# A hybrid attention encoder block on one core: the third block of projection weights is read into the room of the distance table, right behind the fourth tile of tokens

## The chip, the core and the metric

The program runs on one core of one Trainium2 chip, in one launch. Its engines each work through a queue of their own: PE (matrix products; PEld loads the stationary operand), DVE (VectorE), ACT (ScalarE), POOL (GpSimd) and SP (SyncE, which computes nothing here and issues all transfers between memory and on-chip buffers). They meet through semaphores. The metric is the device time of one execution in microseconds (us); lower is better.

## What is computed

One layer of an encoder over 1024 tokens of width 1024 with 16 meta tokens put in front. The part that matters here is the first stage: every token is normalised, and the result is multiplied by pieces of one large weight matrix.

```python
h = jnp.concatenate([meta, x], axis=1)
n = rms_norm(h, norm_mix[layer])
proj = n @ w_in[layer]
qb = proj[..., o:o + QB_W]; o += QB_W
kb = proj[..., o:o + KB_W]; o += KB_W
vb = proj[..., o:o + VB_W]; o += VB_W
y_a = differential_attention(qa, ka, va, ...)
y_b = windowed_gqa(qb, kb, vb, sink)
merged = sigmoid(ga) * (y_a @ w_ba) + sigmoid(gb) * (y_b @ w_bb)
h = h + merged @ w_o
h = h + swiglu(rms_norm(h, norm_ffn), w_gate, w_up, w_down)
```

## The kernel before

**Splitting.** Each float32 operand is split into a high part and a low part (`split`, L116: ACT copies the high part, L117; DVE or POOL subtracts it to get the low part, L118). A product is three passes of PE: high by high, low by high, high by low. The high and the low part of the normalised and transposed tokens stay on chip as `hT_hi` and `hT_lo`.

**The first stage.** There are eight tiles of 128 tokens, called tile 0 to tile 7 here after the buffers `x_0` to `x_7`, and a ninth with the 16 meta tokens. For each tile: `load_x` (L383) has SP issue a read of 512 KB; `norm_x` squares and sums the tile on ACT (L134), takes the root on POOL (L122, L123) and scales on DVE (L140); `turn_x` transposes on PE (L148, eight transposes in two banks) and splits on ACT (L150) and DVE (L151). The "fourth tile" of the title is `x_3`.

**The first three weight blocks.** A block is 128 columns of `w_in`, 512 KB: `kb` (read by `ensure` as `w_c2048`), the first half of `qb` (`w_c1536`), and the second half of `qb`, prepared at L434 under the name `qbx` into a tile of its own, `wb_qbx`, with its low part made on DVE. `project_steps` (L207) multiplies them by the tokens in four chunks of 256 tokens; a chunk needs two tiles. For each chunk PE makes 24 products for `kb` (`pp_kb`), 24 for the first half of `qb` (`pp_qb0`) and 24 for the second (`pp_qb1`), and the calls of `advance` mix these with the transposes of the later tiles. Every finished chunk is split (L232 to L236) and moved by SP to where the attention wants it: eight small transfers for `kb` (L282, sixteen for the last chunk), four for each half of `qb` (L305).

**Buffers.** `prep` (L174) reads a block into a tile of the pool `wpool`, tag `w`, which has two buffers. So the read of `qbx` takes the buffer of `w_c2048` when that has been split, the next block, `w_c2176` (for `vb`), the buffer of `w_c1536`, and the one after, `w_c0` (for the first `qa`), that of `qbx`. The table of distances `dist` (128 x 1920) is allocated and filled at L464 to L473, after all calls of `advance` in the text; DVE and POOL fill it while the projections run.

**After the stage** come the products for `vb` (`pp_vb`), the scores of the windowed attention (`attend_b`; products `bps` at L331, two banks of results, which DVE empties at L333), and the products for `qa` (`pp_qa`), mixed by the planner; then the differential attention, the gates, the output projection and the feed-forward part, which the change does not touch.

**What sets the order.** The instructions of this first part are not executed in the order of the text: a planner with a cost model of its own orders each engine's queue when the program is built. A change in the text can so move instructions it does not name. SP's transfers take eight semaphores in turn: a transfer is issued only after the one eight places ahead of it in the queue has landed. That can be seen where the order lists what an instruction waits for.

Of the kernel before, what the change touches and what calls it, by code (L numbers as in the profile page):

```python
# [9 lines left out]
F32 = mybir.dt.float32  # L10
# [9 lines left out]
P = 128  # L20
S = 1024
D = 1024
NM = 16
L = S + NM
DC = D // P
# [44 lines left out]
C_QA, C_KA, C_VA, C_QB, C_KB, C_VB, C_GA, C_GB = 0, 512, 1024, 1536, 2048, 2176, 2304, 3328  # L70
# [3 lines left out]
def encoder_block(ctx: ExitStack, tc: tile.TileContext, x, meta, norm_mix, w_in, lq1, lk1, lq2, lk2,  # L74
                  subln, sink, w_ba, w_bb, w_o, norm_ffn, w_g, w_u, w_d, norm_final, out, dbg=None):
    nc = tc.nc
    x = x[0]
    out = out[0]
    w_in, w_ba, w_bb, w_o = w_in[0], w_ba[0], w_bb[0], w_o[0]
# [5 lines left out]
    def pool(name, side="left", space=None, bufs=1):  # L85
        kw = {} if space is None else {"space": space}
        if space is not DRAM:
            kw["reuse_waits"] = "tile"
        cm = tc.tile_pool(name=name, bufs=bufs, side=side, **kw)
        p = cm.__enter__()  # L90
        return p, lambda: cm.__exit__(None, None, None)
# [24 lines left out]
    def split(hi, lo, src, lo_eng):  # L116
        nc.scalar.activation(hi, src, AF.Copy)  # L117
        lo_eng.tensor_tensor(lo, src, f32(hi), ALU.subtract)  # L118
# [12 lines left out]
    def normed(p, src, parts, gain, name, tag="xn", bufs=2, on_pool=False):  # L131
        xn = p.tile([P, D], F32, tag=tag, name=f"xn_{name}", bufs=bufs)
        ss = small.tile([P, 1], F32, tag="ss", name=f"ss_{name}")
        nc.scalar.activation(xn[:parts], src, AF.Square, accum_out=ss[:parts])  # L134
        r = rstd_of(ss[:parts], D, parts, f"rstd_{name}")
        if on_pool:
            nc.gpsimd.tensor_scalar(xn[:parts], src, r[:parts], 1.0, ALU.mult, ALU.mult)
            nc.gpsimd.tensor_tensor(xn[:parts], xn[:parts], gain[:parts], ALU.mult)
        else:
            nc.vector.scalar_tensor_tensor(xn[:parts], src, r[:parts], gain[:parts], ALU.mult, ALU.mult)  # L140
        return xn
# [11 lines left out]
    acon, close_acon = pool("acon", "right")  # L153
    hpool, close_hpool = pool("hpool", "right")
    wpool, close_wpool = pool("wpool", "right")
# [15 lines left out]

    queue = []

    def prep(col, name, p=None, lo_eng=None):  # L174
        w = wpool.tile([P, DC, P], F32, tag="w", name=f"w_{name}", bufs=2)
        if isinstance(col, tuple):
            for i, k in enumerate(col):
                nc.sync.dma_start(w[:, 4 * i:4 * i + 4], g_weights(k, 1, 0, P))
        else:
            nc.sync.dma_start(w, w_in[:, col:col + P].rearrange("(c p) n -> p c n", p=P))  # L180
        if p:
            both = p.tile([P, 2, DC, P], F32R, tag="k0", name=f"wb_{name}", bufs=1)
            wh, wl = both[:, 0], both[:, 1]
        else:
            wh = wpool.tile([P, DC, P], F32R, tag="wh", name=f"wh_{name}", bufs=W_BUFS)
            wl = wpool.tile([P, DC, P], F32R, tag="wl", name=f"wl_{name}", bufs=W_BUFS)
        split(wh, wl, w, lo_eng or nc.gpsimd)
        return wh, wl
# [9 lines left out]
    prepped = {}  # L198

    def ensure(n):  # L200
        while order and len(prepped) < n:
            col = order.pop(0)
            prepped[col] = prep(col, f"c{col[0] if isinstance(col, tuple) else col}", lo_eng=nc.vector if col in on_vector else None)
# [60 lines left out]
    lowpool, close_low = pool("lowpool")  # L264
# [115 lines left out]
    def load_x(t):  # L380
        xts[t] = bpool.tile([P, D], F32, tag="btr", name=f"x_{t}", bufs=4)
        if t < NT:
            nc.sync.dma_start(xts[t], x[t * P:(t + 1) * P, :])  # L383
        else:
            nc.sync.dma_start(xts[t][:NM], meta)

    def norm_x(t):
        parts = P if t < NT else NM
        i = len(done)
        done.append(t)  # L390
        p, tag, bufs = (vtpool, "vt", 1) if i % 3 == 2 else (bpool, "bs", 2)
        xns[t] = normed(p, xts.pop(t)[:parts], parts, gmix, f"a{t}", tag=tag, bufs=bufs)

    def turn_x(t):
        parts = P if t < NT else NM
        transposed(lambda name: bank(psum1, ("bt", "bs")[t % 2], name, 2), xns.pop(t), parts, hT_hi, hT_lo, t * P, f"a{t}")
# [29 lines left out]
        nc.tensor.matmul(idle, zeros[:, 0:P], zeros, start=True, stop=True)  # L426
    ensure(2)
    load_x(3)
    norm_x(2)
    turn_x(1)  # L430
    p_kb = project_steps(C_KB, KB_CHUNKS, "kb", evac_split(None, kb_consume))
    p_q0 = qb_steps(0, qb, 0)
    p_q1 = qb_steps(0, qb, 1)
    prepped[C_QB + P] = prep(C_QB + P, "qbx", lowpool, nc.vector)  # L434
    early += [(p_kb, DC), (p_q0, DC), (p_q1, DC)]
    advance(E_STEPS)
    norm_x(3)
# [23 lines left out]
    turn_x(NT)  # L461
    early += [(p_kb, DC), (p_q0, DC), (p_q1, DC)]
    advance(100)
    dist = acon.tile([P, 1920], F32, name="dist")  # L464
    tbx = acon.tile([P, 3, 144], F32, name="tbx")
    for i in range(2):
        cols = slice(960 * i, 960 * i + 960)
# [122 lines left out]
    def g_weights(k, kh, c0, cn):  # L590
        at = (C_GB, C_GA)[k // 4] + k % 4 * 256 + c0
        return w_in[kh * 512:kh * 512 + 512, at:at + cn].rearrange("(c p) n -> p c n", p=P)
# [430 lines left out]
    for o in range(DC):  # L1023
        w = first_w[o] if o < 2 else branch_w(ypool, o, w_bb, "b")
# [424 lines left out]
    for n in range(nf, len(steps)):  # L1449
        p, j = steps[n][1]  # L1450
# [3 lines left out]
        if p in LOADS:  # L1454
            at, half, col = LOADS[p]
# [62 lines left out]
```

## Time and profile before

| what | us |
|---|---|
| time, median of three runs | 1447.92 (1447.72 to 1450.47) |
| time of the profiled execution | 1446.43 |
| its span, first to last instruction | 1444.6 |
| PE busy | 1423.5 (99%) |
| DVE busy | 901.6 (62%) |
| ACT busy | 679.5 (47%) |
| POOL busy | 642.6 (44%) |
| mean granted clock of PE | 0.997 of full speed |

How to read it: the profiled execution is one execution, 1.5 us quicker than the median of the runs beside it, and 1.8 us longer than its own span. PE is busy nearly all the time, so what matters is where PE stands still and for whom. A row of the timeline has the start, the time taken, the engine, the line, the operation and its tiles (written <- read); in brackets the engine's idle time before it and what ended that. Products on PE overlap: the next one starts before the end that is shown for the last.

### The profile page before, as it was taken

To read this page: it belongs to the slowest core of one execution; us is meant where nothing else is said; L and a number is where in the kernel's file an instruction comes from. 1 tells how busy PE (TensorE), PEld (TensorE's weight loads), DVE (VectorE), ACT (ScalarE), POOL (GpSimd) and SP (SyncE) were. 2 spreads that over 40 slices of the span, in tenths; PEclk is the share of its full clock that TensorE was granted. 3 is DMA by queue.
4 is the path that set the end of the run, shared out by engine and by line. 5 is a ranking of instruction groups with operands and counts; after the bars stand their busy time and mean duration, and the time that the engine had idled before them with its cause. 6 is when DMAs were issued, how large, how long until landed. Compare 5 with 4: busy or idle time off the path is not lost.

```text
span 1444.6 us, 21159 instructions
## 1 busy us (share of the span) xinstructions
PE 1423.5 (99%) x7279; PEld 1221.1 (85%) x7279; DVE 901.6 (62%) x1624; ACT 679.5 (47%) x1290; POOL 642.6 (44%) x605
## 2 busy tenths in 40 slices
PE   8999999999999999999999999999999999999997
PEld 6988989988898989888888878888888888888886
DVE  7478536637697989624614966554555553787567
ACT  6356535545665656545413643333333333444454
POOL 5589227743333333334522665544544552000444
PEclk9999999999999999999999999999999999999999
DMA  8367668995558473586602534333332333964343
GB/s 245 87 211 231 195 160 271 283 289 208 189 168 258 147 226 126 190 255 204 224 32 88 152 103 162 110 102 110 101 103 96 110 102 102 334 205 140 124 130 139
DMA packets 188891, 242.41 MB, mean 168 GB/s; under 512 B 18208, under 2 KB 115936, under 8 KB 188784
## 3 DMA queue, kind: packets, MB, share of 16 engines
q1 hardware_dynamic: 188784, 241.07, 52.5%
q8 instruction: 57, 0.93, 0.3%
q14 instruction: 50, 0.41, 0.1%
HBM read 157.45 MB, written 77.00 MB: 162 GB/s over the span
## 4 chain that ended last, share of the span: by engine, by line
PE 80%; POOL 6%; DVE 5%; issue 4%; DMA 3%; ACT 2%; SPq 0%; POOLq 0%; DVEq 0%; ACTq 0%
PE pg L1299 27%; PE pd L1393 9%; PE pg L742 7%; PE ppa L786 6%; PE po L1076 6%; PE aps L802 3%; PE pp_qb L214 3%; PE apy L841 3%; POOL oa L118 3%; PE pp_ka L214 2%; PE pp_va L214 2%; PE apt L828 2%; PE pp_qa L214 2%; PE bpt L356 1%; PE bpy L362 1%
## 5 line engine op out<-in xcount | busy, mean ns | idle before, releaser
L118 POOL TENSOR_TENSOR wop<-wf,wop 128x512 fp32r<-128x512 f32 x128 | 173.5, 1360 | 164.7 <-ACT wop L117 150.3
L1299 PE MATMUL pg<-t,wop 128*128 128x512 f32 x1056 | 242.6, 389 | 0.0
L1299 PEld LDWEIGHTS pg<-t,wop 128*128 128x128 f32 x1056 | 198.2, 188 | 41.2
L1393 PE MATMUL pd<-ob,oa 128*128 128x512 f32 x924 | 209.9, 389 | 0.4 <-POOL oa L118 0.4
L1393 PEld LDWEIGHTS pd<-ob,oa 128*128 128x128 f32 x924 | 173.3, 188 | 36.8 <-POOL oa L118 0.9
L1299 PE MATMUL pg<-b,wop 128*128 128x512 f32 x792 | 185.6, 392 | 2.3 <-DVE c L1308 2.3
L1299 PEld LDWEIGHTS pg<-b,wop 128*128 128x128 f32 x792 | 149.4, 189 | 34.2 <-issue 2.4
L742 PE MATMUL pg<-hT_hi,gop 128*128 128x512 f32 x384 | 142.9, 397 | 0.0
L118 POOL TENSOR_TENSOR oa<-ra,oa 128x512 fp32r<-128x512 f32 x33 | 44.1, 1337 | 170.0 <-ACT oa L117 168.6
L117 ACT ACTIVATE wop<-wf 128x512 fp32r<-128x512 f32 x128 | 80.2, 631 | 83.3 <-PE pg L1299 47.8
L118 POOL TENSOR_TENSOR gop<-gr,gop 128x512 fp32r<-128x512 f32 x47 | 62.0, 1321 | 105.9 <-ACT gop L117 105.9
L117 ACT ACTIVATE oa<-ra 128x512 fp32r<-128x512 f32 x77 | 48.7, 632 | 106.1 <-PE pd L1393 46.0
L810 ACT ACTIVATE as<-as,amn 128x1040 f32<-128x1040 f32 x64 | 74.5, 1165 | 47.3 <-DVE amn L805 43.2
L1134 DVE TENSOR_TENSOR s<-wf,wf 128x512 f32<-128x512 f32 x22 | 23.7, 1077 | 107.6 <-DMA wf<-in_w_ff_gate_dram 57.4
L802 PE MATMUL aps<-ak,aq 128*128 128x392 f32 (+1 forms) x384 | 90.1, 330 | 0.7 <-DVE amn L805 0.4
L1076 PE MATMUL po<-woh,mT 128*128 128x512 f32 x384 | 88.1, 390 | 0.0
L1076 PEld LDWEIGHTS po<-woh,mT 128*128 128x128 f32 x384 | 71.9, 188 | 14.8
L742 PEld LDWEIGHTS pg<-hT_hi,gop 128*128 128x128 f32 x384 | 72.7, 189 | 11.3 <-DVE gk L747 0.2
L802 PEld LDWEIGHTS aps<-ak,aq 128*128 128x128 f32 x384 | 69.6, 189 | 14.3 <-DVE amn L805 2.0
L343 POOL TENSOR_SCALAR bs<-bs,bdn 128x432 f32<-128x432 f32 (+1 forms) x64 | 41.1, 662 | 87.1 <-DVE bdn L341 74.3
L742 PE MATMUL pg<-hT_lo,gop 128*128 128x512 f32 x192 | 76.1, 396 | 0.0
L813 POOL TENSOR_SCALAR as<-as,adn,neglam 128x1040 f32<-128x1040 f32 x32 | 39.1, 1220 | 63.9 <-DVE adn L811 44.6
(289 smaller groups left out, 3105.9 us busy)
## 6 DMA issues: line engine op xcount, KB each, us to landing
ra<-aop SPq DMA_DIRECT2D x77, 256.0 KB, 2.7
wf<-in_w_ff_gate_dram SPq DMA_DIRECT2D x24, 512.0 KB, 3.8
wf<-in_w_ff_up_dram SPq DMA_DIRECT2D x24, 512.0 KB, 3.9
aop<-as SPq DMA_DIRECT2D x44, 256.0 KB, 2.1
w_c<-in_w_in_dram SPq DMA_DIRECT2D x17, 512.0 KB, 6.1
aop<-c SPq DMA_DIRECT2D x33, 256.0 KB, 2.0
ts_d<-to SPq DMA_DIRECT2D x16, 512.0 KB, 3.4
gw<-in_w_in_dram SPq DMA_DIRECT2D x32, 256.0 KB, 4.2
```

The source lines that it names most:

```text
L117: nc.scalar.activation(hi, src, AF.Copy)
L118: lo_eng.tensor_tensor(lo, src, f32(hi), ALU.subtract)
L214: nc.tensor.matmul(ps[:, :n], a[:, c, :], b[:, c, at:at + n], start=(c == 0 and i == 0), stop=(c == DC - 1 and i == 2))
L343: nc.gpsimd.tensor_scalar(st[:, r, :W], st[:, r, :W], dn[:, r:r + 1], 1.0, ALU.mult, ALU.mult)
L742: nc.tensor.matmul(ps, op[:, a, c], quad(b, *act)[:, c], start=(p in (2, 5, 1) and c == 0 and i == 0), stop=(p in (2, 3, 4) and c == 3 and ...
L786: nc.tensor.matmul(ps, w[:, a, j, :], src(j, b, tk), start=(j == 0 and n == 0), stop=(j == 3 and n == 2))
L802: nc.tensor.matmul(ps[:, :n], qs[m][:, t * P:(t + 1) * P], ks[m][:, vv, k0:k0 + n], start=(vv == 0), stop=(vv == 1))
L810: nc.scalar.activation(s[m][:, 0:L], s[m][:, 0:L], AF.Exp, bias=low, scale=-1.0, accum_out=dn[:, m:m + 1])
L841: nc.tensor.matmul(py[:, cols], v[:kp, a, k, :], at_[:kp, k, b, :], start=(k == 0 and j == 0), stop=(k == 8))
L1076: nc.tensor.matmul(ps, mT[:, c, a, t * P:(t + 1) * P], wos[q, c][:, b], start=(c == 0 and n == 0), stop=(c == DC - 1 and n == 2))
L1299: nc.tensor.matmul(ps, op[:, x, c, :], b[:, y, c, :], start=(p in (1, 2, 5) and c == 0 and n == 0), stop=(p in (4, 2, 3) and c == 3 and n ...
L1393: nc.tensor.matmul(ps[u], oa[:, a, u * P:(u + 1) * P], ob[:, b, :], start=(p in (1, 2, 5) and j == 0 and k == 0), stop=(p in (2, 3, 4) and ...
```

## The change

The third block is read by a transfer of its own into the first 1024 columns of `dist`, which is therefore allocated earlier, and that transfer is written right behind `load_x(3)`. `prep` is handed this tile and reads nothing for it; it splits from there as before, ACT for the high part and DVE for the low part. `dist` is filled afterwards as before, once the split has read the block. The third block takes no buffer of the tag `w` any more.

```diff
-    def prep(col, name, p=None, lo_eng=None):
-        w = wpool.tile([P, DC, P], F32, tag="w", name=f"w_{name}", bufs=2)
+    def prep(col, name, p=None, lo_eng=None, w=None):
+        if w is None:
+            w = wpool.tile([P, DC, P], F32, tag="w", name=f"w_{name}", bufs=2)
         if isinstance(col, tuple):
             for i, k in enumerate(col):
                 nc.sync.dma_start(w[:, 4 * i:4 * i + 4], g_weights(k, 1, 0, P))
-        else:
+        elif not p:
             nc.sync.dma_start(w, w_in[:, col:col + P].rearrange("(c p) n -> p c n", p=P))
...
     load_x(3)
+    dist = acon.tile([P, 1920], F32, name="dist")
+    third = dist[:, 0:D].rearrange("p (c n) -> p c n", n=P)
+    nc.sync.dma_start(third, w_in[:, C_QB + P:C_QB + 2 * P].rearrange("(c p) n -> p c n", p=P))
     norm_x(2)
     turn_x(1)
...
-    prepped[C_QB + P] = prep(C_QB + P, "qbx", lowpool, nc.vector)
+    prepped[C_QB + P] = prep(C_QB + P, "qbx", lowpool, nc.vector, third)
...
-    dist = acon.tile([P, 1920], F32, name="dist")
```

The planner answers with another order in the first fifth of the program, on all five engines. Three places follow. Lines of the changed kernel stand a little further down: L384 is L383 of before, L181 is L180, L215 is L214, L234 and L237 are L233 and L236, L332 is L331, and L432 is the new transfer.

**First place: SP's queue behind the fourth tile.** Before:

```order
L383 DMA x_3_241<-in_x_dram 128x1024
L484 DMA gsub_849<-in_subln_gain_dram 128x1
L487 DMA sinkb_852<-in_sink_logits_dram 128x8
L383 DMA x_4_297<-in_x_dram 128x1024
L493 DMA lam_in_857<-in_lambda_q1_dram 128x64
L493 DMA lam_in_857<-in_lambda_k1_dram 128x64
L493 DMA lam_in_857<-in_lambda_q2_dram 128x64
L493 DMA lam_in_857<-in_lambda_k2_dram 128x64
L383 DMA x_5_323<-in_x_dram 128x1024
L180 DMA w_qbx_264<-in_w_in_dram 128x8x128
L180 DMA w_c2176_935<-in_w_in_dram 128x8x128
L383 DMA x_6_349<-in_x_dram 128x1024
```

Now, with what each waits for (the names of the eight transfer semaphores begin with DMAHW):

```order
L384 DMA x_3_241<-in_x_dram 128x1024
L432 DMA dist_243<-in_w_in_dram 128x8x128
L487 DMA gsub_848<-in_subln_gain_dram 128x1 [waits DMAHW0_49]
L490 DMA sinkb_851<-in_sink_logits_dram 128x8 [waits DMAHW1_49]
L384 DMA x_4_297<-in_x_dram 128x1024 [waits DMAHW2_49,DVE_49]
L496 DMA lam_in_856<-in_lambda_q1_dram 128x64 [waits DMAHW3_49,PE_49]
L496 DMA lam_in_856<-in_lambda_k1_dram 128x64 [waits DMAHW4_49]
L496 DMA lam_in_856<-in_lambda_q2_dram 128x64 [waits DMAHW5_49]
L496 DMA lam_in_856<-in_lambda_k2_dram 128x64 [waits DMAHW6_49]
L384 DMA x_5_323<-in_x_dram 128x1024 [waits DMAHW7_49,DVE_49,Activation_49]
L181 DMA w_c2176_934<-in_w_in_dram 128x8x128 [waits DMAHW0_49,Pool_49]
L181 DMA w_c0_1018<-in_w_in_dram 128x8x128 [waits DMAHW1_49,DVE_49]
```

The third block moved from behind `x_5` to behind `x_3`, ahead of `x_4`. The transfer eight places ahead of `x_5` was `x_3` and is now the third block itself. `w_c0`, which stood between the small transfers of the first chunk, now stands ahead of `x_6`; `x_6` and `x_7` follow, `x_7` behind three of the small transfers.

**Second place: PE's and DVE's queue from the transposes of tile 3 to those of tile 5.** PE before, from the second half of tile 3 on (`ptn_a4_1` is the second half of tile 4):

```order
L148 MATMUL ptn_a3_1_313<-ident_109,xn_a3_273 128x128 [waits PE_49]
L148 MATMUL ptn_a3_1_313<-ident_109,xn_a3_273 128x128 x3
L148 MATMUL ptn_a4_0_332<-ident_109,xn_a4_299 128x128 [waits DVE_49]
L148 MATMUL ptn_a4_0_332<-ident_109,xn_a4_299 128x128 x3
L214 MATMUL pp_qb1_0_487<-hT_hi_133,wb_qbx_266 128x256 [waits Activation_49]
L214 MATMUL pp_qb1_0_487<-hT_lo_134,wb_qbx_266 128x256
L148 MATMUL ptn_a4_1_339<-ident_109,xn_a4_299 128x128 [waits DVE_49]
L148 MATMUL ptn_a4_1_339<-ident_109,xn_a4_299 128x128 x3
L214 MATMUL pp_kb_256_519<-hT_hi_133,wh_c2048_192 128x256 [waits DVE_49,Activation_49]
L214 MATMUL pp_qb1_0_487<-hT_hi_133,wb_qbx_266 128x256 [waits DVE_49]
```

PE now, from the end of the products with the third block to the transposes of tile 5:

```order
L215 MATMUL pp_qb1_0_487<-hT_hi_133,wb_qbx_266 128x256
L148 MATMUL ptn_a4_0_332<-ident_109,xn_a4_299 128x128 [waits DVE_49,PE_49]
L148 MATMUL ptn_a4_0_332<-ident_109,xn_a4_299 128x128 x3
L148 MATMUL ptn_a4_1_339<-ident_109,xn_a4_299 128x128 [waits DVE_49]
L148 MATMUL ptn_a4_1_339<-ident_109,xn_a4_299 128x128 x3
L215 MATMUL pp_kb_256_519<-hT_hi_133,wh_c2048_192 128x256 [waits DVE_49,Activation_49]
L215 MATMUL pp_qb0_256_555<-hT_hi_133,wh_c1536_237 128x256 [waits DVE_49]
L148 MATMUL ptn_a5_0_360<-ident_109,xn_a5_325 128x128 [waits DVE_49]
L148 MATMUL ptn_a5_0_360<-ident_109,xn_a5_325 128x128 x3
```

DVE now, in the same stretch:

```order
L140 SCALAR_TENSOR_TENSOR xn_a3_273<-x_3_241,rstd_a3_276,gmix_166 128x1024
L118 TENSOR_TENSOR wb_qbx_266<-dist_243,wb_qbx_266 128x1024
L151 TENSOR_TENSOR hT_lo_134<-ptn_a2_0_280,hT_hi_133 128x4x128
L140 SCALAR_TENSOR_TENSOR xn_a4_299<-x_4_297,rstd_a4_302,gmix_166 128x1024
L151 TENSOR_TENSOR hT_lo_134<-ptn_a2_1_287,hT_hi_133 128x4x128
L234 TENSOR_TENSOR qk_stage_444<-pp_kb_0_269,qk_stage_444 128x256
L237 SCALAR_TENSOR_TENSOR qk_stage_480<-pp_qb0_0_455,qbs_157,qk_stage_480 128x256
L140 SCALAR_TENSOR_TENSOR xn_a5_325<-x_5_323,rstd_a5_328,gmix_166 128x1024
```

The split of the third block (`wb_qbx`) stood behind `xn_a5` on DVE and now stands between `xn_a3` and `xn_a4`. PE takes its first two products with the high part of the block right behind the transposes of tile 2 and the other 22 behind those of tile 3, ahead of tile 4; before, they stood around and behind tile 4. On ACT the square of `x_6` now stands ahead of the eviction of `pp_qb1_0` and of the split of tile 4.

**Third place: the first scores on PE.** Before (`pv_vb` are transposes of `vb`, the numbers behind `bps` the key group, the tile and the head):

```order
L252 MATMUL pv_vb_1_1035<-ident_109,vt_vb_934 128x128 x4
L331 MATMUL bps_0_1_0_905<-kb0_146,qb0_156 128x432 x2
L252 MATMUL pv_vb_2_1044<-ident_109,vt_vb_934 32x128
L331 MATMUL bps_0_1_1_909<-kb0_146,qb0_156 128x432 x2
L331 MATMUL bps_0_1_2_913<-kb0_146,qb0_156 128x432 x2
L331 MATMUL bps_0_1_3_917<-kb0_146,qb0_156 128x432 x2
L331 MATMUL bps_0_2_0_1091<-kb0_146,qb0_156 128x432 x2
L214 MATMUL pp_qa0_0_1645<-hT_hi_133,wh_c0_1021 128x512
```

Now:

```order
L253 MATMUL pv_vb_0_1025<-ident_109,vt_vb_933 128x128 x4
L253 MATMUL pv_vb_1_1034<-ident_109,vt_vb_933 128x128 x2
L332 MATMUL bps_0_0_2_879<-kb0_146,qb0_156 128x288 x2
L332 MATMUL bps_0_0_3_883<-kb0_146,qb0_156 128x288 x2
L253 MATMUL pv_vb_1_1034<-ident_109,vt_vb_933 128x128 x2
L253 MATMUL pv_vb_2_1043<-ident_109,vt_vb_933 32x128
L332 MATMUL bps_0_1_0_904<-kb0_146,qb0_156 128x432 x2
L332 MATMUL bps_0_1_1_908<-kb0_146,qb0_156 128x432 x2
L215 MATMUL pp_qa0_0_1644<-hT_hi_133,wh_c0_1020 128x512
```

Five pairs of scores stood between the transposes of `vb` and the first product for `qa`; now two pairs do, and the next pair follows among the products for `qa`, 22 of them later.

## The prediction, put on record before the change was run

> **What bounds the kernel now.** First the page's busy times, then the waits of PE over the whole span, then the stretches of the first 110 us.
>
> ```profile
> PE 1423.5 (99%) x7279; PEld 1221.1 (85%) x7279; DVE 901.6 (62%) x1624; ACT 679.5 (47%) x1290; POOL 642.6 (44%) x605
> ```
>
> ```profile
> PE ptn_a L148 <- DVE xn_a L140: 2.3, 2, 1.4
> PE pp_qb L214 <- DVE wb_qbx L118: 1.5, 1, 1.5
> ...
> PE bps L331 <- DVE bmn L333: 1.0, 3, 0.5
> ```
>
> ```profile
> 12.00:25.00 13.00, 10.86 (x87) 10.02 (x86) 11.12 (x16) 10.99 (x20) 7.93 (x12) 1.00 0.99 303
> 25.00:40.00 15.00, 15.00 (x130) 14.68 (x130) 14.28 (x23) 7.48 (x17) 7.21 (x8) 1.00 0.53 131
> 40.00:70.00 30.00, 30.00 (x227) 29.89 (x228) 11.03 (x27) 9.63 (x23) 18.15 (x12) 1.00 0.41 89
> ```
>
> PE is the bound: it stands still for only 1444.6 - 1423.5 = 21 us in all. The whole prize of a change that removes no work lies in rows like the second view's (waited for: us, times, longest). The one that the edit names is the second: PE waits once, 1.5 us, for the low part of the third block. The last is the wait at the first scores, which the planner's new order touches. The third view (PE, PEld, DVE, ACT, POOL busy, clock, share of the transfer engines, GB/s) says that until 25 us the transfer engines are full (0.99 at 303 GB/s), and that from 25 to 70 us PE never stops. So order of transfers matters early, and whatever PE gains at 24 us it keeps unless something it meets later is late.
>
> **The removed wait.** The place in the timelines of PE, ACT and DVE:
>
> ```profile
> 20.37 1.47 PE L148 MATMUL ptn_a<-ident,xn_a 128*128 128x128 f32 x12
> 22.28 0.36 PE L214 MATMUL pp_kb<-hT_hi,wh_c 128*128 128x256 f32 x1
> 24.13 0.51 PE L214 MATMUL pp_qb<-hT_hi,wb_qbx 128*128 128x256 f32 x2 [1.50 <-DVE wb_qbx L118]
> 26.83 0.28 PE L214 MATMUL pp_qb<-hT_hi,wh_c 128*128 128x256 f32 x1
> 26.95 0.60 PE L148 MATMUL ptn_a<-ident,xn_a 128*128 128x128 f32 x4
> 19.83 1.07 ACT L117 ACTIVATE wb_qbx<-w_qbx 128x1024 fp32r<-128x1024 f32 x1
> 17.22 1.27 DVE L140 SCALAR_TENSOR_TENSOR xn_a<-x,rstd_a,gmix 128x1024 f32<-128x1024 f32 x1
> 21.67 1.27 DVE L140 SCALAR_TENSOR_TENSOR xn_a<-x,rstd_a,gmix 128x1024 f32<-128x1024 f32 x1
> 22.87 1.21 DVE L118 TENSOR_TENSOR wb_qbx<-w_qbx,wb_qbx 128x1024 fp32r<-128x1024 f32 x1
> ```
>
> The block itself lands in time for ACT at 19.83; its low part is late because DVE scales tile 5 first (21.67). When does the block land after the change? These are SP's issues, and the transfers' times to landing, in the order x_3, x_4, x_5, third block:
>
> ```profile
> 4.27 3.59 SPq L383 DMA_DIRECT2D x<-in_x_dram  x1
> 8.93 0.36 SPq L383 DMA_DIRECT2D x<-in_x_dram  x1
> 14.01 0.33 SPq L383 DMA_DIRECT2D x<-in_x_dram  x1
> 14.44 0.38 SPq L180 DMA_DIRECT2D w_qbx<-in_w_in_dram  x1
> x<-in_x_dram SPq DMA_DIRECT2D x1, 512.0 KB, 9.7
> x<-in_x_dram SPq DMA_DIRECT2D x1, 512.0 KB, 6.4
> x<-in_x_dram SPq DMA_DIRECT2D x1, 512.0 KB, 3.8
> w_qbx<-in_w_in_dram SPq DMA_DIRECT2D x1, 512.0 KB, 5.2
> ```
>
> They landed at 4.27 + 9.7 = 14.0, at 15.3, 17.8 and 19.6. The block streamed in 19.6 - 17.8 = 1.8 us behind x_5, and 512 KB at the 303 GB/s above also take 1.7. Behind x_3 it lands at 14.0 + 1.8 = 15.8, and x_4 is pushed to 15.3 + 1.8 = 17.1. [...] x_5 now waits for the landing eight places ahead, which is the third block: issued at 15.8, it lands at 15.8 + 3.8 = 19.6, 1.8 later than now.
>
> ```profile
> L151 DVE TENSOR_TENSOR hT_lo<-ptn_a,hT_hi 128x512 fp32r<-128x512 f32 (+1 forms) x18 | 10.7, 627 | 2.0 <-ACT hT_hi L150 2.0
> L236 DVE SCALAR_TENSOR_TENSOR qk_stage<-pp_qb,qbs,qk_stage 128x256 fp32r<-128x256 f32 x8 | 3.8, 475 | 4.5 <-ACT qk_stage L235 4.5
> ```
>
> These two groups give the small steps on DVE (0.63 and 0.48 us each). Then ACT makes the high part from 15.8 to 16.9, squares x_4 from 17.1 to 18.3, does tile 2's splits and squares x_5 from about 19.6 to 20.9. DVE in its new order, end to end at full durations: xn_a3 at 17.2 as now, third block's low part 18.5 to 19.7, hT_lo to 20.3, xn_a4 to 21.6, hT_lo to 22.2, two evictions (0.5 at most each) to 23.2, xn_a5 to 24.5. PE: tile 3's transposes at 20.37 plus the two early products with the block (0.24) = 20.6; eight transposes at 0.10 (12 in 1.23) to 21.4; 22 products to 24.1 (24.13 to 26.83 is 2.70); tile 4 to 24.9; two more products, and tile 5's transposes start at 25.2. Now they start at 26.95. **First term: -1.7 us.** Every operand on that list is ready before PE asks: the low part at 19.7 against 21.4, xn_a4 at 21.6 against 24.1, xn_a5 at 24.5 against 25.2. The last margin, 0.7 us, is the thinnest. Bounds: -1.8 (all of 22.28 to 24.13) and 0 (all of it waited for again at tile 5).
>
> **What else moves.** `dist` is filled by the same instructions; on DVE they stand well behind the split that must come first, and DVE's queue is in order, so the new wait costs nothing; if that cover were gone, the table would be late only for the first scores. `w_c0`'s read leaves SP's run of small transfers (0.6 us there) and x_7 enters it (0.4): nothing, since SP is not waited for by PE in that run; bounds -0.6 and +0.6. ACT's queue has a new wait: the square of x_6 stands ahead of the eviction of `pp_qb1_0` and the split of tile 4. x_6 now stands behind x_5, `w_c2176` and `w_c0`: 19.6 + 3 x 1.8 = 25.0. PE needs that eviction's bank only 48 products and tile 5's other half later, near 25.2 + 48 x 0.12 + 0.8 = 31.8. Covered by 5 us.
>
> **The scores.** The rows of PE around that wait:
>
> ```profile
> 69.31 0.64 PE L331 MATMUL bps<-kb,qb 128*128 128x432 f32 x2
> 69.82 0.63 PE L331 MATMUL bps<-kb,qb 128*128 128x432 f32 x2
> 70.72 0.65 PE L331 MATMUL bps<-kb,qb 128*128 128x432 f32 x2 [0.28 <-DVE bmn L333]
> 71.64 0.65 PE L331 MATMUL bps<-kb,qb 128*128 128x432 f32 x2 [0.27 <-DVE bmn L333]
> 72.75 0.67 PE L331 MATMUL bps<-kb,qb 128*128 128x432 f32 x2 [0.46 <-DVE bmn L333]
> 73.26 0.40 PE L214 MATMUL pp_qa<-hT_hi,wh_c 128*128 128x512 f32 x1
> ```
>
> An unhindered pair takes 0.51 (69.31 to 69.82, 72.75 to 73.26). Three pairs took 0.90, 0.92 and 1.11, so the two banks cost PE 2.93 - 1.53 = 1.4. Now two pairs stand there, and the other three among products for `qa`, where DVE has time. But the first of the two follows directly on two others, so I leave one such wait, 0.5. **Second term: -0.9 us.** Bounds: -1.4 and 0 (the wait only moves).
>
> **The sum** is 1.7 + 0.9 = 2.6 us: a span of 1442.0 for an execution like the profiled one. That one took 1446.43, 1.5 less than the median, so the forecast is taken off the median: 1447.92 - 2.6 = **1445.3 us**.
>
> [...] Here the idle times in brackets, 1.5 and 1.0 less one wait of 0.4, would give 2.1 and 1445.8; counted from start to start it is 2.6. [...]
>
> **Rivals.** *All of it goes:* neither tile 5 nor any score waits, and SP's 0.6 brings the next weights earlier: 1.8 + 1.4 + 0.6 = 3.8 at most, 3.3 with half of that 0.6 and a wait of 0.2 left: 1444.6. For it: PE never stops from 25 to 70. Against: two score banks stay two.
>
> *Tile 5 takes the place of the third block.* The root on POOL for each tile:
>
> ```profile
> L122 POOL TENSOR_SCALAR rstd_a<-ss_a x9: 192/192/1175, 5.6 to 30.3; 128x1 f32<-128x1 f32 x8, 16x1 f32<-16x1 f32 x1
> L123 POOL TENSOR_TENSOR rstd_a<-rstd_a,neg_half x9: 551/557/1553, 5.9 to 30.8; 128x1 f32<-128x1 f32 x8, 16x1 f32<-16x1 f32 x1
> 17.48 1.43 POOL L123 TENSOR_TENSOR rstd_a<-rstd_a,neg_half 128x1 f32<-128x1 f32 x1
> ```
>
> The same tiny step took 0.55 or up to 1.55, the long ones (17.48 for 1.43) beside a DVE instruction on two on-chip operands, xn_a at 17.22. With both steps of tile 4 at their worst, its scale factor comes at 18.3 + 1.2 + 1.6 = 21.1 instead of 20.3 at most, and xn_a5 ends at 25.3: the margin is gone, and a landing of x_5 one or two us later than worked out stops PE by nearly as much. With 1.5 of the first term gone: 1446.8. [...]
>
> *The time is lost again at the next weights.* POOL ends the low part of the first `va` block at 83.62 + 2.40, and PE asks for it 2.6 us later:
>
> ```profile
> 83.62 2.40 POOL L118 TENSOR_TENSOR wl_c<-w_c,wh_c 128x1024 fp32r<-128x1024 f32 x1
> 88.61 0.34 PE L214 MATMUL pp_va<-hT_hi,wl_c 128*128 128x384 f32 x1
> ```
>
> If that block came no earlier and most of the rest waited too, 0.5 would remain: 1447.4. Against: POOL's queue is reordered as well, with this split ahead of its neighbours. The same number holds if the read does nothing because SP issues it late.
>
> *Slower:* the square of x_6 holds ACT, and with it the bank that PE needs at 31.8. If `w_c2176`, `w_c0` and x_6 came one after the other at their full median times instead of streaming,
>
> ```profile
> w_c<-in_w_in_dram SPq DMA_DIRECT2D x4, 512.0 KB, 6.8
> x<-in_x_dram SPq DMA_DIRECT2D x8, 512.0 KB, 6.3
> ```
>
> x_6 would land at 19.6 + 6.8 + 6.8 + 6.3 = 39.5, and with square and eviction (1.07 as the ACT row above for as many elements, and some 0.5 for the smaller one) PE would stand 9.2 us: 1447.9 - 2.6 + 9.2 = 1454.5. It decides from a landing of x_6 past 30.3, and makes the kernel slower past 32.9. Against it: at 303 GB/s transfers do stream.
>
> **Chances.** The forecast 0.44, its own range 1444.6 to 1446.2; all of it 0.29; tile 5 0.11; lost again 0.04; slower 0.12. Taken together 8 in 10 lie in 1443.3 to 1448.2: the lower end is the sum of the outer bounds, 3.8, and 0.8 us of scatter; the upper holds "lost again" with the same scatter and leaves the slower case out. About 0.2%, 2.9 us, is what a measurement of this kernel can tell from no change, so faster means below 1445.0. Two fifths of the forecast's chance lie there, and all of the first rival's: faster 0.18 + 0.29 = 0.47, within 0.41, slower 0.12.
>
> **What would show it.** The row of PE's waits for wb_qbx gone; x_4 and x_5 read by ACT at 17.1 and 19.6; tile 5's transposes near 25.2; at the scores one wait rather than three. The first term is wrong if PE waits for tile 5, the second if the waits for L333 again add up to 1.0, both if the order in the later stages brings waits that the list above does not have.

## The result, and the profile after

| | before | changed |
|---|---|---|
| median, 20 runs each, same chip | 1447.82 us (1444.77 to 1451.41) | 1450.59 us (1448.80 to 1453.53) |
| changed over before, 95% interval | | 1.002 (1.0012 to 1.0027) |
| span of the profiled execution | 1444.6 us | 1448.1 us |
| start of the first gate product `pg` (L721 before, L724 changed), from where all engines' orders are the same again | 305.98 us | 308.71 us |

The change makes the kernel 2.8 us slower. The two traces are 3.5 us apart, and 2.7 us of that stands at the first gate product, so most of the loss lies in the part of the program that the planner ordered anew. The page's busy row, the waits of PE over the whole span (waited for: us, times, longest), and the stretches of the first 90 us (PE, PEld, DVE, ACT, POOL busy, clock, share of the transfer engines, GB/s):

```profile
PE 1424.2 (98%) x7279; PEld 1221.1 (84%) x7279; DVE 902.7 (62%) x1624; ACT 679.2 (47%) x1290; POOL 640.7 (44%) x605
```

```profile
PE ptn_a L148 <- DVE xn_a L140: 3.3, 3, 1.3
...
PE pp_vb L215 <- DVE qk_stage L237: 2.3, 1, 2.3
...
PE pp_vb L215 <- POOL wl_c L118: 0.6, 1, 0.6
...
PE bps L332 <- DVE bmn L334: 0.3, 1, 0.3
```

```profile
12.00:25.00 13.00, 12.35 (x102) 11.74 (x101) 11.36 (x15) 9.17 (x17) 7.86 (x10) 1.00 0.97 286
25.00:40.00 15.00, 13.91 (x120) 13.68 (x119) 11.35 (x16) 8.89 (x18) 6.48 (x9) 1.00 0.52 127
40.00:70.00 30.00, 26.74 (x185) 25.72 (x185) 13.87 (x23) 7.12 (x15) 20.12 (x12) 0.94 0.41 87
60.00:65.00 5.00, 4.98 (x20) 4.98 (x21) 0.48 (x1) 0.30 (x1) 3.53 (x2) 0.67 0.42 68
```

The wait for `wb_qbx` is gone and the wait at the scores fell from 1.0 to 0.3 us. (Of the first row, two waits with 2.2 us come ahead of 14 us and stood in the kernel before as well; the third, 1.1 us, is new.) Up to 25 us PE is busy 12.35 us instead of 10.86: 1.5 us ahead. Then come three things that the kernel before did not have: 1.1 us of idle time between 25 and 40 us, 3.3 us between 40 and 70, and inside the latter a clock of 0.67 for five microseconds. The places, in the timelines of PE, SP, ACT, DVE and POOL:

```profile
25.15 0.66 PE L148 MATMUL ptn_a<-ident,xn_a 128*128 128x128 f32 x4
32.95 1.06 PE L148 MATMUL ptn_a<-ident,xn_a 128*128 128x128 f32 x8 [1.09 <-DVE xn_a L140]
56.06 0.34 PE L215 MATMUL pp_vb<-hT_hi,wh_c 128*128 128x384 f32 x1
58.84 0.44 PE L215 MATMUL pp_vb<-hT_hi,wh_c 128*128 128x384 f32 x1 [2.27 <-DVE qk_stage L237]
60.02 0.69 PE L215 MATMUL pp_vb<-hT_hi,wl_c 128*128 128x384 f32 x1 [0.57 <-POOL wl_c L118]
17.35 3.66 SPq L384 DMA_DIRECT2D x<-in_x_dram  x1
21.11 1.06 ACT L134 ACTIVATE xn_a<-x 128x1024 f32<-128x1024 f32 x1 [1.28 <-DMA x<-in_x_dram]
27.72 1.06 ACT L134 ACTIVATE xn_a<-x 128x1024 f32<-128x1024 f32 x1 [4.12 <-DMA x<-in_x_dram]
57.79 0.47 ACT L236 ACTIVATE qk_stage<-pp_qb,qbs 128x256 fp32r<-128x256 f32 x1 [1.62 <-DMA qb<-qk_stage]
29.27 0.48 DVE L237 SCALAR_TENSOR_TENSOR qk_stage<-pp_qb,qbs,qk_stage 128x256 fp32r<-128x256 f32 x1 [3.58 <-ACT qk_stage L236]
42.26 1.27 DVE L151 TENSOR_TENSOR hT_lo<-ptn_a,hT_hi 128x512 fp32r<-128x512 f32 x2
43.02 2.17 POOL L529 TENSOR_TENSOR tal<-hT_lo 128x512 f32<-128x512 f32 x1 [4.54 <-DVE hT_lo L151]
57.62 2.35 POOL L118 TENSOR_TENSOR wl_c<-w_c,wh_c 128x1024 fp32r<-128x1024 f32 x1
```

Read from the top: tile 5's transposes start at 25.15, as predicted. SP issues x_6 at 17.35, behind `w_c0`, and the issue itself takes 3.66 us. ACT stands 4.12 us for x_6, until 27.72, with an eviction behind it in its queue, and DVE stands 3.58 us for that eviction. PE then waits 1.09 us for tile 6. Tile 7 is late too (its last transfer completes at 30.8 us instead of 26.2). Behind its 3.58 us DVE has next to no idle time (0.07 us) until it splits tile 7, at 42.26 instead of 38.03. The token sums on POOL, which read tiles 4 to 7, wait for that split and start at 43.02 instead of 38.78. The rows below show how the lateness reaches the value block `vb`. In the kernel before:

```profile
38.03 0.67 DVE L151 TENSOR_TENSOR hT_lo<-ptn_a,hT_hi 128x512 fp32r<-128x512 f32 x1
38.78 1.27 POOL L526 TENSOR_TENSOR tal<-hT_lo 128x512 f32<-128x512 f32 x1 [1.68 <-DVE hT_lo L151]
53.79 4.76 POOL L118 TENSOR_TENSOR wl_c<-w_c,wh_c 128x1024 fp32r<-128x1024 f32 x2
54.75 0.48 DVE L236 SCALAR_TENSOR_TENSOR qk_stage<-pp_qb,qbs,qk_stage 128x256 fp32r<-128x256 f32 x1 [2.45 <-ACT qk_stage L235]
56.40 0.33 PE L214 MATMUL pp_vb<-hT_hi,wh_c 128*128 128x384 f32 x1
56.74 0.33 PE L214 MATMUL pp_vb<-hT_hi,wl_c 128*128 128x384 f32 x1
```

Two things join at `pp_vb`. The third product needs the bank that DVE's eviction frees: free at 54.75 + 0.48 = 55.2, used at 56.40, 1.2 us to spare. The fifth needs the block's low part from POOL: made at 53.79 + 2.4 = 56.2, used at 56.74, **0.5 us to spare**. After the change PE comes at the same time (56.06 against 56.04), but the eviction comes at 58.30 and the low part at 60.0.

Time from the start of one product to the start of the next, summed by group from the trace up to the first gate product, shows the whole account in us:

| products of | before | changed | difference |
|---|---|---|---|
| key and query blocks (`pp_kb`, `pp_qb`, 384 in all) | 60.2 | 60.2 | -0.1 |
| value block (`pp_vb`) | 11.4 | 16.3 | +4.9 |
| scores and what follows them (`bps`, `bpt`, `bpy`) | 72.2 | 68.9 | -3.3 |
| all others, with the 1.2 us ahead of the first | 162.1 | 163.4 | +1.2 |
| sum | 306.0 | 308.7 | +2.7 |

The first row hides two parts: the 1.5 us that were gained up to 25 us, and the 1.5 us that tile 6 and the small tile cost behind it. Of the 4.9 us at `pp_vb`, 3.2 are the two waits, counted from start to start, and the rest is the half clock.

Behind the first gate product the two traces go apart by another 0.8 us, although every engine's order is the same there. The changed kernel falls back by 1.6 us near 470 us, at scores of the other attention (`aps`), and catches up 1.1 us near 836 us, where only the kernel before has a drop of the clock (3.41 us at half clock from 834.6 us on). The waits at `aps` between 400 and 500 us, before and after:

```profile
PE aps L802 <- DVE amn L805: 0.4, 1, 0.4
```

```profile
PE aps L805 <- DVE amn L808: 1.3, 1, 1.3
...
PE aps L805 <- DVE at L835: 0.2, 1, 0.2
```

That is not the change: in the traces of e4 and e12 below, which start from the kernel before, PE waits some 1.5 us there too. The trace of the kernel before was a lucky one at this place.

### The profile page after: what moved, and what is told of

It is laid out like the page before. It is cut to its first block, busy times and chain, and to the rows that moved or that the text cites. A ratio compares the mean times of both kernels' runs of the same rounds, so it can differ in the third digit from the quotient of the medians.

```text
span 1448.1 us, 21167 instructions
## 1 busy us (share of the span) xinstructions
PE 1424.2 (98%) x7279; PEld 1221.1 (84%) x7279; DVE 902.7 (62%) x1624; ACT 679.2 (47%) x1290; POOL 640.7 (44%) x605
## 4 chain that ended last, share of the span: by engine, by line
PE 82%; POOL 4%; issue 4%; DMA 3%; DVE 3%; ACT 2%; SPq 1%; POOLq 0%; ACTq 0%; DVEq 0%
PE pg L1302 27%; PE pd L1396 9%; PE pg L745 8%; PE ppa L789 6%; PE po L1079 6%; PE aps L805 3%; PE pp_ka L215 3%; PE pp_va L215 3%; PE pp_qa L215 3%; PE apy L844 3%; POOL oa L118 3%; PE apt L831 2%; PE bpt L357 2%; PE bpy L363 2%; PE pp_qb L215 2%
## 5 line engine op out<-in xcount | busy, mean ns | idle before, releaser
L1137 DVE TENSOR_TENSOR s<-wf,wf 128x512 f32<-128x512 f32 x22 | 24.5, 1114 | 106.5 <-DMA wf<-in_w_ff_gate_dram 57.1
L1079 PEld LDWEIGHTS po<-woh,mT 128*128 128x128 f32 x384 | 71.9, 188 | 14.8
```

The source lines that it names most:

```text
L1079: nc.tensor.matmul(ps, mT[:, c, a, t * P:(t + 1) * P], wos[q, c][:, b], start=(c == 0 and n == 0), stop=(c == DC - 1 and n == 2))
```

## The experiments

A copy of one element on POOL, from a tile of split tokens into the first element of a weight tile, makes that weight's read wait; this is the tool in most of them. "Null" means that such a copy was added and every engine's order stayed as it was.

**e1 and e2: `w_c0` held.** The edit, with 384 (tile 3) in e1 and 512 (tile 4) in e2:

```diff
         elif not p:
+            if col == C_QA:
+                nc.gpsimd.tensor_copy(w[0:1, 0, 0:1], f32(hT_lo)[0:1, DC - 1, 512:513])
             nc.sync.dma_start(w, w_in[:, col:col + P].rearrange("(c p) n -> p c n", p=P))
```

> The changed kernel with one row moved on SP: the read of the query block w_c0 (freed early, because the third block no longer takes a turn in its pool) stands right behind the read of x_6 instead of right ahead of it; a copy of one element on POOL holds it there, and the other orders differ from the changed kernel's only up to about 45 us. Theory (w_c0 ahead of x_6 is what costs): x_6 is in at 24 to 26 us instead of 27.6, ACT no longer waits 4.1 us for it, the 1.1 us of PE ahead of tile 6 goes, the 2.8 us at the first products of pp_vb shrinks under 1, and the clock stays at 1.00 between 60 and 65 us: 1445 to 1447.5 us. Rival 1 (the third read's own 0.5 MB makes everything behind it late, whatever the order): x_6 is in after 27 us all the same and the time stays at 1450 to 1451. Rival 2 (the planner's later order of scores and token sums costs, not the landing): x_6 is early, the waits at pp_vb stay at 2 to 3 us, 1449 to 1451.

> The changed kernel with w_c0 held until tile 4 has been split: SP then reads it behind all stores of kb and qb, at about 60 us, and neither ahead of x_6 nor of x_7. Theory: x_6 in at 24 to 26, x_7 in at 26 to 28 instead of 30.8, SP's stores 2 to 3 us earlier than in the changed kernel, no wait over 1 us at pp_vb; 1444.5 to 1447, unless the block is now late for its own products behind pp_vb, which would show as a wait of PE at pp_qa. Rival 1: x_6 after 27, 1450 to 1451. Rival 2: 1449 to 1451.

Measured 1451.11 us, ratio 1.0021 (1.0012 to 1.003), and 1449.89 us, 1.0015 (1.0006 to 1.0024). In e1's run SP did not have `w_c0` right behind x_6 as its text says, but behind all stores, as in e2: the two runs are one order taken twice. Their waits of PE in e2:

```profile
PE bps L332 <- DVE bmn L334: 1.5, 3, 0.8
PE pp_vb L215 <- DVE qk_stage L237: 1.2, 1, 1.2
...
PE pp_vb L215 <- POOL wl_c L118: 0.6, 1, 0.6
PE pp_qa L215 <- ACT wh_c L117: 0.6, 1, 0.6
```

```profile
25.00:40.00 15.00, 15.00 (x130) 14.68 (x129) 13.18 (x19) 9.41 (x20) 6.94 (x10) 1.00 0.47 120
```

With x_6 in at 25.0 the wait at tile 6 is gone (15.00 of 15.00 busy), and PE is at `pp_vb` at 54.4, 1.7 us before the kernel before. There it waits 1.9 us. The order at the scores is also another one, with 1.5 us of waits at the scores and 0.6 for `w_c0`, now late itself. So the first half of the theory holds (x_6 early, no wait at the tile) and its time does not; the edit moved too much to tell more.

**e3: the release alone.** The block still goes to the table's room, but its read is held:

```diff
-    nc.sync.dma_start(third, w_in[:, C_QB + P:C_QB + 2 * P].rearrange("(c p) n -> p c n", p=P))
...
+    nc.gpsimd.tensor_copy(third[0:1, 0, 0:1], f32(hT_lo)[0:1, DC - 1, 0:1])
+    nc.sync.dma_start(third, w_in[:, C_QB + P:C_QB + 2 * P].rearrange("(c p) n -> p c n", p=P))
     prepped[C_QB + P] = prep(C_QB + P, "qbx", lowpool, nc.vector, third)
```

> The third block is read into the distance table's room, so that w_c0's read is freed early as in the changed kernel, but its read is held by a copy of one element on POOL until tile 0 has been split, so that it goes behind x_5 and w_c2176 on SP: the pool's release without the early read. Theory: x_6 is late (27 us or more), ACT waits for it with the evictions behind it, and the first wait of PE for wb_qbx is back and longer than the 1.5 us of before (the block lands 2 us later than there, behind w_c2176): 1450 to 1454. Rival 1 (the early read costs): x_4 and x_5 land as before, x_6 as before, 1447 to 1449.

Measured 1450.81 us, 1.0018 (1.0008 to 1.0028). Waits of PE, and ACT's row for x_6:

```profile
PE pp_vb L214 <- POOL wl_c L118: 2.1, 1, 2.1
PE ptn_a L148 <- DVE xn_a L140: 2.1, 3, 0.9
...
PE pp_qb L214 <- ACT wb_qbx L117: 1.3, 1, 1.3
```

```profile
28.38 1.06 ACT L134 ACTIVATE xn_a<-x 128x1024 f32<-128x1024 f32 x1 [3.31 <-DMA x<-in_x_dram]
```

Without the early read, but with `w_c0` ahead of x_6, the time is as long: x_6 at 28.3, the block waited for again (1.3 us), 2.1 us at `pp_vb`. (Two of the three waits in the second row, 1.8 us, come ahead of 14 us, as in every run.) So the loss does not need the early read, which speaks against rival 1. The test is not a clean one, since the old wait for the block came back with it; e9 below, which keeps the early read, is the better one.

**e4: null on the kernel before.** The edit of e2 in the kernel before.

> The kernel before with the same copy of one element on POOL ahead of w_c0's read, held until tile 4 has been split: every engine's order is that of the kernel before, w_c0's read stands at its old place between the stores of qb, and only the copy on POOL is added. All theories: 1447 to 1448.7, no difference from before; a difference over 1 us would say that the copy itself costs.

1447.95 us, 1.0001 (0.9992 to 1.0011). The copy costs nothing, and two traces of that order have `pg` at 305.98 and 305.76.

**e5, e7, e8: half of qb's stores from ACT's queue**, on the changed kernel (e5), on the one before (e7), and on the changed one with the value block's low half on DVE (e8, the edit of e6):

```diff
-                    nc.sync.dma_start(f32(qb)[64 * hl:64 * hl + 64, 2 * jj + par, at:at + n],
+                    (nc.sync, nc.scalar)[hl].dma_start(f32(qb)[64 * hl:64 * hl + 64, 2 * jj + par, at:at + n],
```

> The changed kernel with half of qb's stores (those of the low part) issued from ACT's queue instead of SP's: 24 of SP's 88 small stores of kb and qb go, at some 0.65 us each. New theory after the first runs (SP's store run sets the pace: in the changed kernel SP's 48th store goes out at 58.4 us against 55.3 before, the last evictions of pp_qb wait for a staging buffer, and PE at pp_vb waits for their bank): the 2.3 us wait of PE for qk_stage at pp_vb goes or falls under 0.5, the clock stays full there (the drop of 3.4 us at half clock cost 1.7), the first product of the gates (pg) starts at 305 to 307 us instead of 308.7, and the run takes 1446 to 1448.5. Rival (the late tile x_6 and DVE's and ACT's own order set it, not the stores): the wait stays over 1.5 us, pg starts at 308 or later, 1449.5 to 1451. The planner's order of scores behind it can move by 1 to 2 us either way and is read from the rows bps to pp_va.

> The kernel before with the same half of qb's stores on ACT's queue. Store theory: before, PE comes to pp_vb 1.2 us after its bank is free, so less work on SP buys nothing there; wb_qbx's 1.5 us and the three short waits at the scores stay: pg at 305 to 306.5, 1447 to 1448.5. Rival (stores cost time in the kernel before as well): 1445 to 1446.5.

> The changed kernel with both: half of qb's stores on ACT's queue and the value block's low half on DVE. Store theory: no wait over 0.5 us at pp_vb, no drop of the clock there, the early gain of about 1.5 us (less 1.5 for x_6) kept and the better order of scores kept (2 us): pg at 303.5 to 306, 1444 to 1447.5. Rival: as the changed kernel, 1449.5 to 1451.

Measured 1451.81 (1.0024, 1.0014 to 1.0034), 1452.01 (1.0028, 1.0017 to 1.0039) and 1451.41 us (1.0029, 1.002 to 1.0038). In e5 and e8 the waits at `pp_vb` did go, but others came in their place, and e7 shows that the edit costs 4 us where there was nothing to mend. The largest wait in e5 and in e7 (between 20 and 100 us):

```profile
PE ptn_a L148 <- DVE xn_a L140: 2.6, 1, 2.6
```

```profile
PE bps L331 <- DVE bmn L333: 3.1, 2, 2.4
```

Inconclusive on the stores: ACT's own work and the planner's order moved with them.

**e6, e10, e12: the value block's low half on DVE**, in the changed kernel (e6 in one run, e10 in twelve) and in the one before (e12):

```diff
-    on_vector = order[on_vector:] + [C_QB, (0, 1), (2, 3)]
+    on_vector = order[on_vector:] + [C_QB, C_VB, (0, 1), (2, 3)]
```

> The changed kernel with one instruction moved: the low half of the value block (wl of w_c2176) is made on DVE instead of POOL; all other orders are as in the changed kernel. Store theory: the wait of 0.6 us for wl_c at pp_vb goes, the 2.3 us for qk_stage stays, so pg starts 0.5 to 0.7 us earlier (308.0 to 308.3), or 2.2 us earlier if the wait is then too short for the clock to drop. Rival (POOL's token sums are what is late): the qk_stage wait shrinks too, pg at 306 or earlier.

> e6's kernel again, now timed in rounds: the value block's low half on DVE, everything else as in the changed kernel. If e6's one look holds (pg at 304.8, no drop of the clock at pp_vb): 1446 to 1448. If it was the luck of one execution (x_6 was in 0.75 us earlier than in the changed kernel's profile): 1449.3 to 1450.6.

> The kernel before with the value block's low half on DVE instead of POOL. There PE has no wait at pp_vb, so the move alone is worth nothing at that place: 1447 to 1448.3, pg at 305.5 to 306.2. If it gains over 1 us, e6's gain is not the change's loss undone but a gain of its own.

e6 gave 1447.94 us in its one run and `pg` at 304.8; e10, the same kernel, 1449.82 us, 1.0013 (1.0001 to 1.0025), and `pg` at 306.2; e12 1447.74 us, 1.0001 (0.9991 to 1.001). The waits at `pp_vb` fall to 0.3 us in both traces of the changed kernel, so POOL's late low part is a real part of them. What e10 has left is the tile:

```profile
PE ptn_a L148 <- DVE xn_a L140: 2.6, 2, 2.4
...
PE pp_vb L215 <- DVE qk_stage L234: 0.3, 1, 0.3
```

There x_6 came at 29.0, in e6 at 26.9: the same order, and 2 us apart from one execution to the next. e6's single run was partly luck. The edit is worth 1 us at most (1.0013 against 1.002, and the intervals overlap).

**e9 and e15: one row on SP.** Held until tile 1 has been split (e9), `w_c0`'s read moves by one place, right behind x_6; other orders differ only up to 45 us. Held until tile 0 (e15), nothing moves: the null of the changed kernel.

```diff
+            if col == C_QA:
+                nc.gpsimd.tensor_copy(w[0:1, 0, 0:1], f32(hT_lo)[0:1, DC - 2, 128:129])
```

> The changed kernel with the copy of one element on POOL holding w_c0's read until tile 1 has been split, so that SP issues it one place later, right behind x_6 (e1 and e2, held longer, both had it behind all stores, and the planner's later order changed with it); the orders are the changed kernel's but for some 50 products of PE and 30 rows of the other engines up to 45 us. Theory 1 (w_c0 ahead of x_6 makes the tile late, and the evictions, stores and token sums behind it): x_6 in by 26.3 us, no wait over 0.5 us at tile 6, pp_vb's waits down from 2.8 to under 1.5 us together and no drop of the clock: gates (pg) start at 305 to 307 us, 1447 to 1449. Theory 2 (x_6's extra time is in the slowest DMA engine's tail and not in the order): x_6 in after 26.3 and pg at 308 to 309, 1449.5 to 1451.

> The changed kernel with the copy of one element on POOL but held only until tile 0 has been split: all orders are the changed kernel's, w_c0 ahead of x_6. All theories: as the changed kernel, 1449.5 to 1451.5, x_6 in after 26.5 us, waits of 2 us or more at pp_vb and pg at 308 to 309.5. If it is 1448.5 or less, e9's gain is the copy's and not the order's.

e9: 1448.59 us, **1.000 (0.999 to 1.0009)**. e15: 1451.21 us, **1.003 (1.0019 to 1.0041)**. Neither interval touches the other, and e9's lies below the changed kernel's own. ACT's row for x_6 and PE's waits in e9:

```profile
26.09 1.06 ACT L134 ACTIVATE xn_a<-x 128x1024 f32<-128x1024 f32 x1 [2.19 <-DVE hT_lo L151]
```

```profile
PE pp_vb L215 <- POOL wl_c L118: 1.2, 1, 1.2
PE pp_vb L215 <- DVE qk_stage L237: 1.0, 1, 1.0
PE ptn_a L148 <- DVE xn_a L140: 0.9, 1, 0.9
```

By the times, one place in SP's queue is worth the loss. x_6 is in 1.6 us sooner than in the changed kernel's profile, and tile 6 is not waited for; the 0.9 us is at tile 7. `pp_vb` still waits 2.2 us (under 1.5 was expected), and that eats the early gain, so that e9 is level with the kernel before and not ahead of it. The waits at `pp_vb` in e15:

```profile
PE pp_vb L215 <- DVE qk_stage L237: 1.6, 1, 1.6
PE pp_vb L215 <- POOL wl_c L118: 1.2, 1, 1.2
```

The traces show less of the difference than the times. `pg` starts at 306.5 us in e9 and at 306.9 in e15, where 308 to 309.5 was expected. e15's traced execution was the quickest of its ten (1448.86 us): it waits at `pp_vb` as long as the changed kernel, but the clock did not drop there (1.00 from 56 to 70 us). So of the 2.6 us between the medians the two traces show some 0.4 as waiting. The mean clocks of the two sets of runs differ by 0.0012, which would be 1.7 us if all of it cost time; that share is worked out, not shown.

**e11, e13, e14: more of the same.** e11 is e9 with the DVE edit. e13 holds both weight blocks, so that x_6 stands right behind x_5; e14 is e13 with the DVE edit.

```diff
+            if col in (C_VB, C_QA):
+                at = 128
+                nc.gpsimd.tensor_copy(w[0:1, 0, 0:1], f32(hT_lo)[0:1, DC - 2, at:at + 1])
```

> w_c0 right behind x_6 (e9) and the value block's low half on DVE (e10) together. If both costs are real and apart: 1444.5 to 1447, pg at 303 to 305. If only the DVE half is: as e10. If neither: 1449.5 to 1451.

> As e9, with a second copy of one element that holds w_c2176's read as well, so that SP reads x_6 right behind x_5 and ahead of both weight blocks; every other order is e9's. Theory 1 (the late tile is the whole loss): x_6 in by 24.5 us, no wait at tile 6, the evictions and stores a further 1 to 1.5 us earlier, waits at pp_vb under 1.2 us together, pg at 304 to 305.8, 1445.5 to 1448. Theory 2 (what is left is a cost of the changed order): x_6 early, but pp_vb's waits stay at 2 us or more, pg at 306 to 307, 1448 to 1449.5.

> e13 with the value block's low half on DVE. Theory 1: no wait over 0.5 us at pp_vb, the early 1.7 us and the better order of scores both kept, pg at 303 to 305, 1444.5 to 1447, faster than the kernel before. Theory 2: as e11, pg at 305.5 to 306.6, 1448 to 1450.

Measured 1449.85 (1.0014, 1.0005 to 1.0023), 1448.89 (1.0011, 1.0002 to 1.0019) and 1449.53 us (1.0019, 1.0009 to 1.0028). In e13 x_6 is squared as early as in the kernel before, and yet:

```profile
19.03 4.11 SPq L387 DMA_DIRECT2D x<-in_meta_tokens_dram  x1
30.05 1.06 ACT L134 ACTIVATE xn_a<-x 128x1024 f32<-128x1024 f32 x1 [3.86 <-DMA x<-in_x_dram]
56.22 0.47 ACT L237 ACTIVATE qk_stage<-pp_qb,qbs 128x256 fp32r<-128x256 f32 x1 [0.77 <-DMA qb<-qk_stage]
```

```profile
PE pp_vb L216 <- DVE qk_stage L238: 1.6, 1, 1.6
PE pp_vb L216 <- DVE qk_stage L235: 0.3, 1, 0.3
```

The lateness went one tile further. SP's issue of the small tile takes 4.11 us with two weight blocks ahead of it, x_7 is read at 30.05 instead of 26.27, and SP sends the 49th of the small stores at 57.3 us, against 55.3 before and 58.4 in the changed kernel. The last evictions wait for those stores to free a staging buffer, and PE, 1 us early, waits for the evictions. Behind its wait for tile 7's root (2.84 us) DVE has no idle time until it splits tile 7, at 40.28 us. In e11 and e14 the waits at `pp_vb` fall to 0.4 and 0.5 us, but DVE, which makes the low part there, is late for PE at 104 us in both; in e14:

```profile
PE bpy L364 <- DVE btr L362: 1.6, 1, 1.6
```

No version beat the kernel before. e11 and e14 missed the gain hoped for (1447 us or less); e13's time is in the range of its second theory and its `pg`, 305.6, in that of the first.

## Why the prediction was wrong, by its own steps

- **Landing and order up to tile 5: right.** x_4 was expected at 17.1 and read at 17.26; the low part was to end at 19.7 and ended at 18.61 + 1.22 = 19.8; xn_a5 was to end at 24.5 and did; tile 5's transposes were to start at 25.2 and started at 25.15. x_5 came 1.5 us later than the 19.6 worked out, and it cost nothing. The rival of tile 5 did not come.
- **"Whatever PE gains at 24 us it keeps unless something it meets later is late": the step that failed.** It was taken from PE's own rows, which show no wait between 25 and 70 us. The spare time of what joins PE there was not read: 0.5 us for POOL's low part and 1.2 us for the bank at `pp_vb`. Even if nothing had come later than before, 1.7 us could not have been kept without waiting there.
- **"`w_c0`'s read leaves SP's run ... nothing", bounds ±0.6: mis-sized.** It was priced as SP's issue time. What counts is that its 512 KB then stand ahead of x_6 and x_7. e9 gives the size: 2.0 us between the medians of e9 and the changed kernel (1450.59 - 1448.59), 2.6 against its null. The size is not firm: e11 and e13, where x_6 comes earlier still, keep a ratio of 1.0014 and 1.0011, so e9 alone is level.
- **"x_6 ... 25.0. Covered by 5 us": wrong twice.** It came at 27.6, and it came at 29.0 and 26.9 in the same order again. And the cover was counted for one user only, the bank at 31.8. Tile 6's own transposes asked first (1.1 us), and the lateness of tiles 6 and 7 went on through DVE, POOL's token sums and SP's stores to `pp_vb`.
- **The slower rival** had the right mechanism, x_6's square holding ACT behind `w_c0`, but put the point from which it decides at a landing of 30.3 or later. The changed kernel is slower at 27.6 already.
- **The scores: right in sign, too small.** -0.9 was forecast; the waits fell by 0.7, and by the table above the scores and what follows them took 3.3 us less. This was not worth its full size either, since it only filled part of the hole at `pp_vb`.
- **The clock was left out.** Over all timed runs beside these experiments the mean granted clock was 0.9979 in 121 runs of the kernel before and 0.9968 in the 20 of the changed one. (Each run's value has three decimals.) The difference, 0.0011 of 1448 us, is 1.6 us of PE's clock. In the profile it is the row with 0.67, and cost some 1.5 of the 2.7 us there (16.3 us at `pp_vb` against 14.8 in e15, which has the same waits and no drop). e9's runs have 0.9978, e15's 0.9966, which goes the same way. As an estimate, then, up to 1.6 of the 2.8 us is clock and the rest is waiting; it is rather too high, since not every drop costs its full 1.7 us (see the last section).

What stays open: e13 brings `pg` to 305.6, earlier than e9's 306.5, and is not faster (its runs have a mean clock of 0.9965). Its trace shows where the time goes: near 470 us, in the part whose order no run changes, PE waits 3.0 us at `aps`, against 0.4 in the trace of the kernel before and some 1.5 in e4's and e12's. Why it waits longer there was not settled. Timed runs leave no trace, so where their clock drops fall, and why this order draws more of them, was not settled either.

Of the two ways to `pp_vb`, the traces settle the one over the token sums. In the changed kernel, e1, e2, e9, e13 and e15 POOL ends the low part 17.6 to 17.7 us after DVE begins to split tile 7, whether that is at 39.7 us (e2) or at 42.3: what is late there arrives late by as much. With the low half on DVE (e6, e11, e14) PE comes to `pp_vb` at 55.1 to 55.8 us and waits 0.3 to 0.5 us; with it on POOL (the changed kernel, e9, e13, e15) it comes at 55.0 to 56.1 and waits 2.0 to 2.9. The part of the stores in the wait for the bank stays open: e5, e7 and e8 moved too much else.

## What to carry to other kernels

Before crediting a gain at one place, read the spare time at every later join of the engine that gains: a row without a wait says nothing about how near the wait is, and the smallest spare time caps what is kept. Taking a tile out of a rotating pool is a change of its own: the next user of that slot is released earlier and its transfer may go ahead of something that is needed sooner. Move such a release one place at a time, with a null beside it; here those two runs told what larger edits had not.

## What the runs showed of the hardware

**A drop of the clock lasted 3.41 us, and what it cost depended on its place.** In the traces' clock records each drop lasts 3.41 us at half clock, which takes 1.7 us of work (3.41 x 0.5) from a PE that is never idle. (One, in e11, lasted 6.83, and in the kernel before and the changed one another begins some 2.4 us ahead of the span's end and outlasts it.) At `pp_vb` it cost some 1.5 us, as worked out above. Near 836 us, where all orders are the same, the changed kernel, without it, gained 1.1 us on the kernel before, with it. Near 340 us executions without it were 1.5 us ahead at 345 us, but then waited for DVE (2.0 us at `aps` in e2), and by 360 us only 0.2 were left. In the kernel before and the changed one each drop of 3.41 us began 0.7 to 1.8 us after the end of a pause of PE, but not every pause was followed by one: near 340 us, where PE waits 1.2 to 1.9 us ahead of transposes of the other attention (`apt`), it came in 10 of the 17 profiles; near 836 us, where PE waits 1.9 to 2.0 us at products of the feed-forward part (also named `pg`), in 11 of 17, the kernel before (2.01 us) among them and the changed one (2.01 us) not. At `pp_vb` it followed waits of 2.3 and 0.6 us in the changed kernel, of 2.1 in e3, of 1.3 and 0.8 in e1, and not those of 1.6 and 1.2 in e15. What decides whether a drop follows is not shown.

**The last part of a read came up to 3.1 us after its first.** For x_6 the first and the last completion of the engines that share the transfer lay 1.3 us apart in the kernel before (22.1 to 23.4) and 3.1 us in the changed kernel (24.6 to 27.6) and in e15 (24.2 to 27.3). In the changed kernel fifteen of the sixteen were in by 26.7 us, and the last alone took another 1.0. The landing worked out from bytes and GB/s, 25.0, came near the first of these.

**In two traces the issue of x_6 ended with the landing of x_5.** It took 1.10 us in the kernel before and 3.66 us in the changed one, where those of x_4, x_5 and x_7 took 0.33 to 0.54, and it ended at 17.83 and 21.01 us; x_5 landed at 17.85 and 21.03. In e9 it took 0.49 us and ended at 17.31, 4.1 us before ACT had x_5 (21.42). What held it is not shown.

**Stores beside instruction packets took longer to issue.** The trace has a 16 KB instruction packet at 50.75 us (1.27 us long) in the changed kernel, and the store issued at 50.64 takes 1.78 us where its neighbours take 0.60; in the kernel before, the packet is at 50.64 and the store at 50.65 takes 1.40. The same pair stands near 22 and 36 us in both, with stores of 1.08 to 1.62 us. That the store waits for the packet is not shown, only that the two come together.
